# A hybrid decoder layer on one core: v's transposition leaves TensorE for VectorE blocks and DRAM transfers, and a head's delta rule starts at another step

## The chip, the cores and the metric

One core of one Trainium2 chip runs the whole program. The metric is the device time of one execution in microseconds. The kernel before takes 2156.06 us, the median of three runs that lie between 2155.36 and 2157.12 us.

## The reference, cut to what matters

One decoder layer works on 512 prompt tokens and 8 single sample tokens of width 2048. The part that the change touches is the prompt's gated delta rule: 8 heads of 128 columns, of which q, k and v come out of one input projection, a short causal convolution over time and a SiLU.

```python
qkv_c, new_conv = short_conv(conv_buf, qkv, conv_w)      # 4 taps over time, then silu
q = l2norm(q) * (DN_HEAD_DIM ** -0.5)
k = l2norm(k)
...
def step(S, xs):                                          # chunk by chunk, in order
    q_i, k_i, u_i, w_i, g_i, qk_i = xs
    v_new = u_i - jnp.einsum('bhck,bhkv->bhcv', w_i, S)
    o = (jnp.einsum('bhck,bhkv->bhcv', q_i * jnp.exp(g_i)[..., None], S)
         + jnp.einsum('bhcs,bhsv->bhcv', qk_i, v_new))
    S = S * jnp.exp(g_last)[..., None, None] + jnp.einsum('bhck,bhcv->bhkv', k_dec, v_new)
    return S, o
```

Beside it stand a pooling group, the output projection and a SwiGLU feed-forward network, whose matrices take most of the time. Everything is float32.

## The kernel before, in words

The program has a first phase up to about 605 us (input projection, convolution, delta rule, pooling) and then the output projection and the feed-forward network. Only the first phase is changed.

**Projection tiles.** `product` computes 128 columns of the input projection for all tokens. The weights are split into a high and a low part, and each of the 16 k tiles takes three matmuls for each of two halves of the tokens (lines 168 to 170, 256 or 264 columns wide): 96 matmuls a tile. The halves are skewed by three k tiles. The weights come in granules of eight k tiles: `raw` by DMA on SP's queue, `hi` cast on ScalarE (line 135), `lo` subtracted on VectorE (line 137), each with three buffers. `to_columns` (line 259) scales a finished half out of PSUM into `ext`; four VectorE operations (lines 737 and 739) make the convolution `y`, and ScalarE the SiLU (line 740).

**The weave.** Everything that is not a projection is cut into generators. `Weave.step()` is called after every k tile of a product from the fourth on and once at its end, 16 times a product; it advances up to four tracks. A generator yields how many steps its track then rests, and `add` takes the steps it waits before it starts. A track runs its tasks strictly one after the other: track 0 has the delta rule and, after it, the sample tokens' work; track 1 gates, keys and the pooling products; track 2 the transpositions over DRAM; track 3 the gates of the output. TensorE's instructions stand in this hand-made order. On VectorE, ScalarE and GpSimd a scheduler sorts them by its own estimate of when they can run, and each engine works its list strictly in order.

**A head.** `qv_tiles(h)` makes q's tile, then v's. Five steps after q's tile, `query_rows` turns q by 32x32 blocks on VectorE (line 753) into `bt`, writes it to DRAM from GpSimd's queue, and six steps later reads it back with four transfers into `qk`, whose rows are tokens. ScalarE squares these rows (line 923) for q's norm. `delta(h)` is added after v's tile and starts one step later. In it `it` 0 to 2 build a triangular inverse `cur` (matmuls of line 870, VectorE's line 872). At `it` 1 TensorE turns v by four transposes (line 885), and VectorE multiplies the rows by `ik` out of PSUM into `vs` (line 887). Then four chunks follow in order. In each, TensorE makes `wp` from `R` (line 904), ScalarE copies it to `W` (906), TensorE makes `dp` from `W` (909), VectorE makes the state `S` (912 or 914), TensorE makes `kp` from `S` (897), and VectorE the next `R` (899). At the end `on` is made from PSUM (939), and six steps later `output_columns` turns it back with a block transposition (764), one transfer to DRAM and four from it, on the same track 2 and the same GpSimd queue. Heads 0 to 3 and 4 to 7 are two batches; after each come other tiles (keys, or the pool's).

**The end of the phase.** After head 7, eight `pool_tile` products follow, and under them track 0 runs head 7's delta rule, then the sample tokens. The last of these, `sample_out`, multiplies its result into `mixa` (line 1015). The output projection then halves `mixa` (line 203), splits 16 tiles into high and low (line 195), and multiplies them (lines 1176 to 1178).

Of the kernel before, what the change touches and what calls it, by code (L numbers as in the profile page):

```python
# [8 lines left out]
F32 = mybir.dt.float32  # L9
# [3 lines left out]
ALU = mybir.AluOpType  # L13
# [4 lines left out]
P = 128  # L18
# [3 lines left out]
SEQ = 512  # L22
NTOK = NB + SEQ
H = 8
NCH = 4
# [8 lines left out]
HG = 8  # L34
BUFS = {
    "ext": 2, "y": 1, "ys": 1, "g3": 3, "junk": 1, "ss": 2, "rr": 2, "nb": 1, "u": 1, "tm": 2, "xt_": 1, "uu": 2,
    "qts": 1, "fq": 2, "aq": 1, "vs": 1, "bt": 2, "tq": 1, "R": 2, "W": 2, "S": 2, "so": 2, "ro": 2, "s0": 2, "s2": 1, "kd": 4, "st": 2,
}
SKEW = 3
AHEAD = 2000  # L40
# [29 lines left out]
def decoder_kernel(ctx, tc, x_prompt, x_sample, state_delta, state_conv, state_pool, norm_mix, w_in,  # L70
# [4 lines left out]
    te, act, dve, pool, sp = nc.tensor, nc.scalar, nc.vector, nc.gpsimd, nc.sync  # L75
# [12 lines left out]
    def pst():  # L88
        return ps_dn.tile([P, 512], F32, tag="dn", name="dn")
# [31 lines left out]
    weave = Weave()  # L121
# [399 lines left out]
    with ExitStack() as p1:  # L521
# [4 lines left out]
        def d1tile(tag, shape, name, dtype=F32):  # L526
            return (pre if tag == "ext" else d1).tile(shape, dtype, tag=tag, name=name, bufs=BUFS[tag])
# [192 lines left out]
        def v3(a):  # L720
            return a.rearrange("p (c j) -> p c j", c=NCH)

        def bc3(a):
            return a.rearrange("p (c o) -> p c o", o=1).broadcast_to([P, NCH, P])

        def ck(c):
            return slice(P * c, P * (c + 1))
# [12 lines left out]
            act.activation(out, y, AF.Silu)  # L740
            pool.tensor_copy(ccp[:, :, t], ext[:, SEQ:SEQ + 3])

        tok_d = dram.tile([2, H, P, SEQ], F32, name="tok_d")

        def by_chunk(a):
            return a.rearrange("p (i c q) -> p c i q", i=4, c=NCH)

        def by_column(a):
            return a.rearrange("p (i q) -> p i q", i=4)

        def query_rows(h, qT):
            bt, d = d1tile("bt", [P, SEQ], "bt"), tok_d[0, h]
            dve.transpose(bt.rearrange("p (j c q) -> p c j q", j=4, c=NCH), qT.rearrange("p (c j q) -> p c j q", j=4, c=NCH))
            pool.dma_start(d, bt)
            yield 6
            rows = d.rearrange("(i p) (j f) -> j p i f", p=32, j=4)
            qk = qks[h] = d1tile("tq", [P, SEQ], "qk")
            for j in range(4):
                pool.dma_start(qk[32 * j:32 * j + 32, :].rearrange("p (n q) -> p n q", n=4), rows[j])

        def output_columns(h, on):
            bt = d1tile("bt", [P, SEQ], "bt")
# [80 lines left out]
            yield 1  # L843


        def delta(h, qT, vT):
            kT, nn, kd = mixb[:, h % 4, 0:SEQ], mixb[:, 4 + h % 4, 0:SEQ], kds[h]
            fk, ik = sck[:, h, 0, :], sck[:, h, 1, :]
            utf = utfs[h % 2]
            udf, tdf = utf[:, 0], utf[:, 1]  # L850
            gcb, dm = decay(h)
            act.activation(gcb, gcb, AF.Exp)
            qts = d1tile("qts", [P, SEQ], "qts")
            dve.tensor_tensor(qts, qT, gcb, op=ALU.mult)

            xp = pst()
            for c in range(NCH):
                te.matmul(xp[:, P * c:P * c + 96], nn[:, ck(c)], tdf[:, c, 0:96], start=True, stop=True)  # L860
            xt_ = d1tile("xt_", [P, NCH, 96], "xt_")
            act.copy(xt_, v3(xp)[:, :, 0:96])
            cur = d1tile("uu", [P, SEQ], "uu")
            pool.tensor_copy(v3(cur), udf)
            yield 2
            for it in range(3):
                yp = v3(pst())
                j = slice(32 * it + 32, P)
                for c in range(NCH):
                    te.matmul(yp[0:96, c, j], xt_[:, c, :], udf[:, c, j] if it == 0 else v3(cur)[:, c, j],  # L870
                              start=True, stop=True)
                dve.scalar_tensor_tensor(v3(cur)[0:96, :, j], yp[0:96, :, j], -1.0, udf[0:96, :, j],
                                         op0=ALU.mult, op1=ALU.add)
                if it == 0:
                    gq_ = pst()
                    for c in range(NCH):
                        te.matmul(gq_[:, ck(c)], kT[:, ck(c)], qT[:, ck(c)], start=True, stop=True)
                    aq = d1tile("aq", [P, SEQ], "aq")
                    for c in range(NCH):
                        dve.scalar_tensor_tensor(aq[:, ck(c)], gq_[:, ck(c)], fk[:, c:c + 1], dm[:, ck(c)],  # L880
                                                 op0=ALU.mult, op1=ALU.mult)
                if it == 1:
                    vtp = pst()
                    for c in range(NCH):
                        te.transpose(vtp[:, ck(c)], vT[:, ck(c)], ident)
                    vs = d1tile("vs", [P, SEQ], "vs")
                    dve.tensor_tensor(v3(vs), v3(vtp), bc3(ik), op=ALU.mult)
                yield 2

            op_ = pst()  # L890
            S = None
            for c in range(NCH):
                if S is None:
                    R = vs[:, ck(c)]
                else:
                    kp = pst()
                    te.matmul(kp[:, 0:P], kT[:, ck(c)], S, start=True, stop=True)
                    Rt = d1tile("R", [P, P], "R")
                    dve.scalar_tensor_tensor(Rt, kp[:, 0:P], negc[:, c, h:h + 1], vs[:, ck(c)],
                                             op0=ALU.mult, op1=ALU.add)  # L900
                    R = Rt
                    yield 2
                wp = pst()
                te.matmul(wp[:, 0:P], cur[:, ck(c)], R, start=True, stop=True)
                W = d1tile("W", [P, P], "W")
                act.copy(W, wp[:, 0:P])
                yield 2
                dp = pst()
                te.matmul(dp[:, 0:P], kd[:, ck(c)], W, start=True, stop=True)
                S2 = d1tile("S", [P, P], "S")  # L910
                if S is None:
                    dve.tensor_copy(S2, dp[:, 0:P])
                else:
                    dve.scalar_tensor_tensor(S2, S, egl[:, c, h:h + 1], dp[:, 0:P], op0=ALU.mult, op1=ALU.add)
                    te.matmul(op_[:, ck(c)], qts[:, ck(c)], S, start=True, stop=False)
                te.matmul(op_[:, ck(c)], aq[:, ck(c)], W, start=(S is None), stop=True)
                S = S2
                yield 1
                if c == 0:
                    ss = d1tile("ss", [P, NCH], "ss")  # L920
                    junk = d1tile("junk", [P, P], "junk")
                    for j in range(NCH):
                        act.activation(by_column(junk), by_chunk(qks[h])[:, j], AF.Square, accum_out=ss[:, j:j + 1])
# [11 lines left out]
            dve.tensor_scalar(so, so, 1.0 / P, EPS, op0=ALU.mult, op1=ALU.add)  # L935
# [179 lines left out]
        def qv_tiles(h):  # L1115
            utf = utfs[h % 2].rearrange("p a c j -> p (a c) j")
            for q in range(4):
                r = slice(32 * q, 32 * q + 32)
                sp.dma_start(utf[r, :, r], ud_d[h, q].rearrange("a c s j -> s (a c) j"))
            qT = d1tile("s0", [P, SEQ], "qT")  # L1120
            qkv_tile(0, h, qT)
            weave.add(query_rows(h, qT), 2, 5)
            vT = d1tile("s2", [P, SEQ], "vT")
            qkv_tile(2, h, vT)
            weave.add(delta(h, qT, vT), 0, 1)

        kds, qks = {}, {}
        for b in range(2):
# [17 lines left out]
        splits = {}  # L1146
# [11 lines left out]
        for t in (6, 7, 4, 5, 2, 3, 0, 1):  # L1158
            pool_tile(t, operands)
            if t % 2:  # L1160
                weave.add(pool_mix(t // 2, *splits[t // 2]), 1, 20 if t == 7 else 12 if t > 1 else 7)
        weave.add(pool_out(), 0, 6)

        order = [*range(8), 14, 15, 12, 13, 10, 11, 8, 9]
# [939 lines left out]
```

## Time and profile before

| what | value |
|---|---|
| median of 3 runs | 2156.06 us (2155.36 to 2157.12) |
| the profiled execution | 2156.18 us, span 2154.4 us |
| TensorE busy, of the span | 99% |
| VectorE, ScalarE, GpSimd busy | 82%, 43%, 22% |
| granted TensorE clock | 1.00 |

TensorE's row is full from the first slices to the end. Its matmuls overlap, so a matmul "of 0.28 us" starts 0.12 us after the one before it: what an instruction costs TensorE is read from the starts of its neighbours, not from its own length. Waits of the other engines cost nothing by themselves as long as TensorE's next instruction has its operands.

### The profile page before, as it was taken

What the parts mean: (1) busy time and instruction counts of PE and PEld (TensorE: products, weight loads), DVE (VectorE), ACT (ScalarE), POOL (GpSimd) and SP (SyncE); (2) the same over time, 40 slices, a digit from 0 to 9 for tenths busy, and PEclk for the clock granted to TensorE, in tenths of its full rate; (3) what the DMA queues carried; (4) which work ended last, traced back from release to release, by engine and by line L of the source; (5) the groups of instructions that cost most, each with busy time, mean ns of one, the idle gap of its engine ahead of it and who ended that gap; (6) DMA issues with size and microseconds to landing.
All of it is one profiled execution on the core that took longest, in us unless ns stands there. A gap on an engine that the chain in (4) does not pass through costs nothing.

```text
span 2154.4 us, 43035 instructions
## 1 busy us (share of the span) xinstructions
PE 2129.6 (99%) x17745; PEld 2121.1 (98%) x17745; DVE 1759.6 (82%) x2635; ACT 929.0 (43%) x1404; POOL 481.9 (22%) x592
## 2 busy tenths in 40 slices
PE   8999999999999999999999999999999999999998
PEld 7999999999999999999999999999999999999998
DVE  7786767666599979888888888888887897887997
ACT  6533452433255454434434434434334444435444
POOL 2112320231012202333233233232113302003100
PEclk9999999999999999999999999999999999999999
DMA  8344434443445534454455455454456746438333
GB/s 282 92 121 110 116 103 117 115 117 98 128 126 166 152 105 124 144 170 144 137 172 147 134 172 147 134 172 133 118 148 195 228 111 205 115 104 247 93 108 119
DMA packets 445826, 305.44 MB, mean 142 GB/s; under 512 B 27836, under 2 KB 424533, under 8 KB 442285
## 3 DMA queue, kind: packets, MB, share of 16 engines
q1 hardware_dynamic: 422733, 219.94, 36.5%
q0 software_dynamic: 21584, 81.95, 12.0%
q8 instruction: 139, 2.28, 0.4%
q10 hardware_dynamic: 1312, 0.80, 0.1%
q14 instruction: 58, 0.48, 0.1%
HBM read 255.66 MB, written 47.63 MB: 141 GB/s over the span
## 4 chain that ended last, share of the span: by engine, by line
PE 85%; DVE 8%; DMA 2%; ACT 2%; issue 2%; POOL 1%; DVEq 0%; ACTq 0%; POOLq 0%; SPq 0%
PE dn L1250 21%; PE dn L1249 21%; PE dn L1251 21%; PE mm L168 6%; PE mm L170 5%; PE mm L169 5%; DVE lo L1243 1%; DVE lo L137 1%; PE dn L870 1%; DMA st<-a_d 1%; DVE raw L1271 1%; POOL st L1803 0%; DVE tm L836 0%; PE dn L986 0%; DVE u L838 0%
## 5 line engine op out<-in xcount | busy, mean ns | idle before, releaser
L1243 DVE TENSOR_TENSOR lo<-raw,hi 128x1024 fp32r<-128x1024 f32 (+1 forms) x422 | 528.6, 1272 | 89.5 <-ACT hi L1242 87.4
L1242 ACT CAST hi<-raw 128x1024 fp32r<-128x1024 f32 (+1 forms) x422 | 427.5, 1027 | 402.9 <-DVE raw L1271 204.2
L168 PE MATMUL mm<-xh,hi 128*128 128x256 f32 (+1 forms) x1280 | 379.5, 297 | 2.6 <-DVE mixa L259 2.6
L169 PE MATMUL mm<-xl,hi 128*128 128x256 f32 (+1 forms) x1280 | 361.6, 283 | 0.9 <-DVE xl L350 0.5
L170 PE MATMUL mm<-xh,lo 128*128 128x256 f32 (+1 forms) x1280 | 361.7, 283 | 0.4 <-DVE lo L137 0.4
L168 PEld LDWEIGHTS mm<-xh,hi 128*128 128x128 f32 x1280 | 241.4, 189 | 3.8 <-DVE mixa L259 3.2
L169 PEld LDWEIGHTS mm<-xl,hi 128*128 128x128 f32 x1280 | 241.7, 189 | 1.7 <-DVE xl L350 1.7
L170 PEld LDWEIGHTS mm<-xh,lo 128*128 128x128 f32 x1280 | 240.9, 188 | 0.6 <-DVE lo L137 0.6
L1271 DVE TENSOR_TENSOR raw<-raw 128x1024 f32<-128x1024 f32 (+1 forms) x130 | 174.6, 1343 | 2.2
L1250 PE MATMUL dn<-b21l,hi 128*128 128x260 f32 x620 | 175.8, 284 | 0.4 <-DVE b21l L1813 0.4
L1251 PE MATMUL dn<-b21h,lo 128*128 128x260 f32 x620 | 175.4, 283 | 0.0
L1249 PE MATMUL dn<-b21h,hi 128*128 128x260 f32 x620 | 174.9, 282 | 0.0
L1251 PE MATMUL dn<-b11h,lo 128*128 128x260 f32 x612 | 173.2, 283 | 1.4 <-DVE lo L1243 1.4
L1250 PE MATMUL dn<-b11l,hi 128*128 128x260 f32 x612 | 173.3, 283 | 0.0
L1249 PE MATMUL dn<-b11h,hi 128*128 128x260 f32 x612 | 172.7, 282 | 0.0
L1435 POOL TENSOR_TENSOR mixa<-mixa 128x520 f32<-128x520 f32 x22 | 51.3, 2330 | 495.5 <-DVE mixa L1429 495.5
L1249 PE MATMUL dn<-T1h,hi 128*128 128x260 f32 x556 | 158.1, 284 | 0.0
L1250 PE MATMUL dn<-T1l,hi 128*128 128x260 f32 x556 | 157.7, 284 | 0.0
L1251 PE MATMUL dn<-T1h,lo 128*128 128x260 f32 x556 | 156.7, 282 | 0.0
L1249 PE MATMUL dn<-B22h,hi 128*128 128x260 f32 x548 | 155.9, 284 | 0.0
L1250 PE MATMUL dn<-B22l,hi 128*128 128x260 f32 x548 | 155.6, 284 | 0.0
L1251 PE MATMUL dn<-B22h,lo 128*128 128x260 f32 x548 | 154.6, 282 | 0.4 <-DVE lo L1243 0.4
(663 smaller groups left out, 6504.0 us busy)
## 6 DMA issues: line engine op xcount, KB each, us to landing
raw<-in_w_gate_up_dram SPq DMA_DIRECT2D x134, 512.0 KB
raw<-in_w_in_dram SPq DMA_DIRECT2D x79, 512.0 KB
a_d<-mixa POOLq DMA_DIRECT2D x22, 1040.0 KB, 5.5
raw<-in_w_down_dram SPq DMA_DIRECT2D x48, 448.0 KB
mixb<-in_w_gate_up_dram SPq DMA_DIRECT2D x41, 512.0 KB
raw<-in_w_out_dram SPq DMA_DIRECT2D x25, 512.0 KB
st<-a_d POOLq DMA_DIRECT2D x49, 260.0 KB, 6.8
raw<-in_w_down_dram SPq DMA_DIRECT2D x24, 512.0 KB
```

The costliest lines, as they stand in the source:

```text
L137: dve.tensor_tensor(lo[:, r], raw[:, r], hi[:, r].bitcast(F32), op=ALU.subtract)
L168: te.matmul(acc[ci], wh, hi[k][:, c0:c1], start=(k == 0), stop=False)
L169: te.matmul(acc[ci], wh, lo[k][:, c0:c1], start=False, stop=False)
L170: te.matmul(acc[ci], wl, hi[k][:, c0:c1], start=False, stop=(k == len(w) - 1))
L870: te.matmul(yp[0:96, c, j], xt_[:, c, :], udf[:, c, j] if it == 0 else v3(cur)[:, c, j], start=True, stop=True)
L1242: act.copy(hi, raw)
L1243: dve.tensor_tensor(lo, raw, hi.bitcast(F32), op=ALU.subtract)
L1249: te.matmul(acc, wh[:, k, :], xf[:, k, :], start=start and k == 0, stop=False)
L1250: te.matmul(acc, wh[:, k, :], xg[:, k, :], start=False, stop=False)
L1251: te.matmul(acc, wl[:, k, :], xf[:, k, :], start=False, stop=stop and k == wh.shape[1] - 1)
L1271: dve.tensor_tensor(r[name], r[a], r[b], op=op)
L1435: pool.tensor_tensor(q[:, 4:8:2, :], q[:, 1:4:2, :], q[:, 0:2, :], op=ALU.subtract)
```

## The change

v's tile goes ahead of q's. `query_rows` becomes `token_rows(kind, h, src, dst)`, and v goes through it too: a block transposition, one transfer to a third plane of `tok_d`, and four transfers back, now into `vs` itself, whose SiLU output they overwrite. The four transposes on TensorE and their PSUM bank are gone. The multiplication by `ik` is done in place in SBUF at `it` 1 (`scaled`). `vs` is laid out by column blocks, so the first `wp` and the `R` of later chunks read it in four pieces of 32 columns. `vs` has two buffers. The delta rule starts eight weave steps after q's tile instead of one after v's, and the pool product of the first pool pair waits 34 steps in place of 20.

```diff
-    "qts": 1, "fq": 2, "aq": 1, "vs": 1, ...
+    "qts": 1, "fq": 2, "aq": 1, "vs": 2, ...
-        tok_d = dram.tile([2, H, P, SEQ], F32, name="tok_d")
+        tok_d = dram.tile([3, H, P, SEQ], F32, name="tok_d")
+        def scaled(a, s):
+            a = a.rearrange("p (i c q) -> p i c q", i=4, c=NCH)
+            dve.tensor_tensor(a, a, s.rearrange("p (o c u) -> p o c u", o=1, u=1).broadcast_to([P, 4, NCH, 32]),
+                              op=ALU.mult)
-        def query_rows(h, qT):
-            bt, d = d1tile("bt", [P, SEQ], "bt"), tok_d[0, h]
-            dve.transpose(bt.rearrange(...), qT.rearrange(...))
+        def token_rows(kind, h, src, dst):
+            bt, d = d1tile("bt", [P, SEQ], "bt"), tok_d[kind, h]
+            dve.transpose(bt.rearrange(...), src.rearrange(...))
             pool.dma_start(d, bt)
             yield 6
             rows = d.rearrange("(i p) (j f) -> j p i f", p=32, j=4)
-            qk = qks[h] = d1tile("tq", [P, SEQ], "qk")
+            if dst is None:
+                dst = qks[h] = d1tile("tq", [P, SEQ], "qk")
             for j in range(4):
-                pool.dma_start(qk[32 * j:32 * j + 32, :].rearrange("p (n q) -> p n q", n=4), rows[j])
+                pool.dma_start(dst[32 * j:32 * j + 32, :].rearrange("p (n q) -> p n q", n=4), rows[j])
 ...
                 if it == 1:
-                    vtp = pst()
-                    for c in range(NCH):
-                        te.transpose(vtp[:, ck(c)], vT[:, ck(c)], ident)
-                    vs = d1tile("vs", [P, SEQ], "vs")
-                    dve.tensor_tensor(v3(vs), v3(vtp), bc3(ik), op=ALU.mult)
+                    scaled(vs, ik)
 ...
-                    R = vs[:, ck(c)]
+                    R = by_chunk(vs)[:, c]
-                    dve.scalar_tensor_tensor(Rt, kp[:, 0:P], negc[:, c, h:h + 1], vs[:, ck(c)],
-                                             op0=ALU.mult, op1=ALU.add)
+                    dve.scalar_tensor_tensor(by_column(Rt), by_column(kp[:, 0:P]), negc[:, c, h:h + 1],
+                                             by_chunk(vs)[:, c], op0=ALU.mult, op1=ALU.add)
 ...
+            vs = d1tile("vs", [P, SEQ], "vs")
+            qkv_tile(2, h, vs)
+            weave.add(token_rows(2, h, vs, vs), 2, 5)
             qT = d1tile("s0", [P, SEQ], "qT")
             qkv_tile(0, h, qT)
-            weave.add(query_rows(h, qT), 2, 5)
-            vT = d1tile("s2", [P, SEQ], "vT")
-            qkv_tile(2, h, vT)
-            weave.add(delta(h, qT, vT), 0, 1)
+            weave.add(token_rows(0, h, qT, None), 2, 5)
+            weave.add(delta(h, qT, vs), 0, 8)
 ...
-                weave.add(pool_mix(t // 2, *splits[t // 2]), 1, 20 if t == 7 else 12 if t > 1 else 7)
+                weave.add(pool_mix(t // 2, *splits[t // 2]), 1, 34 if t == 7 else 12 if t > 1 else 7)
```

The changed kernel's lines stand three higher in the delta rule (line 915 is the old 912) and seven higher where q is turned.

**VectorE, the first chunk of head 1.** Before, from the last step of the inverse (`uu`) to the first `R`; `S` is the state after chunk 0, `lo` a weight granule, `mixa` the gate of the head before:

```order
L872 SCALAR_TENSOR_TENSOR uu<-dn,utf_647 96x4x32
L927 TENSOR_SCALAR fq<-fq 128x4
L933 TENSOR_TENSOR ro<-fq 128x4
L137 TENSOR_TENSOR lo<-raw,hi 128x1024
L944 SCALAR_TENSOR_TENSOR mixa<-mixb,prm,mixa 128x512
L912 COPY S<-dn 128x128
L899 SCALAR_TENSOR_TENSOR R<-dn,negc,vs 128x128
```

and now:

```order
L879 SCALAR_TENSOR_TENSOR uu<-dn,utf_647 96x4x32
L259 TENSOR_TENSOR ext<-mm,rb 128x256
L737 TENSOR_SCALAR y<-ext,prm 128x512
L137 TENSOR_TENSOR lo<-raw,hi 128x1024
L739 SCALAR_TENSOR_TENSOR y<-ext,prm,y 128x512
L927 TENSOR_SCALAR ss<-ss 128x4
L739 SCALAR_TENSOR_TENSOR y<-ext,prm,y 128x512
L915 COPY S<-dn 128x128
L739 SCALAR_TENSOR_TENSOR y<-ext,prm,y 128x512
L930 TENSOR_SCALAR fq<-fq 128x4
L902 SCALAR_TENSOR_TENSOR R<-dn,negc,vs 128x128
```

Between the inverse and `S` now stand an eviction, three of the four convolution operations of the next head's v, a weight granule, and `ss`, which needs ScalarE's squares of `qk`. Heads 1, 2, 3, 5 and 6 have this order; head 7 has the pool's additions in place of the convolution. On TensorE the distance from the matmul of `dp` to that of `kp`, which reads `S`, is 6 projection matmuls before and now; from the first `wp` to `dp` it was 12 and is 21.

**GpSimd, one head.** The transfers of head 1 before (`qk` is head 2's q, `mixb` head 1's output):

```order
L754 DMA tok_d<-bt 128x512
L759 DMA qk<-tok_d 32x4x128 x4
L864 COPY uu<-utf_647 128x512
L215 TENSOR_TENSOR ro<-so,mhalf 128x4
L741 COPY ccp<-ext 128x3
L765 DMA tok_d<-bt 128x4x128
L769 DMA mixb<-tok_d 32x16x32 x4
L215 TENSOR_TENSOR fq<-ss,mhalf 128x4
```

and now (`qk` is head 1's q, `mixb` head 0's output, `vs` head 2's v):

```order
L215 TENSOR_TENSOR ro<-so,mhalf 128x4
L760 DMA tok_d<-bt 128x512
L772 DMA tok_d<-bt 128x4x128
L766 DMA qk<-tok_d 32x4x128 x4
L776 DMA mixb<-tok_d 32x16x32 x3
L741 COPY ccp<-ext 128x3
L776 DMA mixb<-tok_d 32x16x32
L215 TENSOR_TENSOR fq<-ss,mhalf 128x4
L263 MEMSET ext 128x3
L760 DMA tok_d<-bt 128x512
L766 DMA vs<-tok_d 32x4x128 x4
```

The order has five more transfers a head, and the write of the output stands between q's write and q's reads. In ScalarE's order the first two of the four squares of `qk` now stand, in all eight heads, ahead of a weight cast `hi` and of the first `W`; before they stood around the copy of `xt_`, ahead of the inverse.

**VectorE, the end of the phase.** From the sample tokens' last matmul (its result is read by the first row) to the product into `mixa`, before:

```order
L1012 TENSOR_SCALAR sc_u<-dn 128x64
L137 TENSOR_TENSOR lo<-raw,hi 128x1024
L220 RECIPROCAL sc_u<-sc_u 128x64
...
L259 TENSOR_TENSOR pe_7259<-mm,rb 128x256
L259 TENSOR_TENSOR pcs<-mm,rb 128x8
...
L1015 SCALAR_TENSOR_TENSOR mixa<-sc_u,prm,mixa 128x8x8
L203 TENSOR_TENSOR mixa<-mixa 128x4x260 x2
```

and now:

```order
L1015 TENSOR_SCALAR sc_u<-dn 128x64
...
L1077 TENSOR_TENSOR pes<-pe_7256 128x512
L137 TENSOR_TENSOR lo<-raw,hi 128x1024 x2
L220 RECIPROCAL sc_u<-sc_u 128x64
...
L1082 SCALAR_TENSOR_TENSOR pw<-pes,pe_7256 128x512
...
L195 TENSOR_TENSOR dl<-pw,dh 128x520
L1018 SCALAR_TENSOR_TENSOR mixa<-sc_u,prm,mixa 128x8x8
L203 TENSOR_TENSOR mixa<-mixa 128x4x260 x2
```

One pool addition, a second weight granule, `pw` and `dl` are now ahead of it, and on TensorE 102 projection and pool matmuls stand between that last sample matmul and the output projection, where it was 153.

More of the change, by code (lines that the diff above doesn't have):

```diff
@@ L36 @@
     "ext": 2, "y": 1, "ys": 1, "g3": 3, "junk": 1, "ss": 2, "rr": 2, "nb": 1, "u": 1, "tm": 2, "xt_": 1, "uu": 2,
-    "qts": 1, "fq": 2, "aq": 1, "vs": 1, "bt": 2, "tq": 1, "R": 2, "W": 2, "S": 2, "so": 2, "ro": 2, "s0": 2, "s2": 1, "kd": 4, "st": 2,
+    "qts": 1, "fq": 2, "aq": 1, "vs": 2, "bt": 2, "tq": 1, "R": 2, "W": 2, "S": 2, "so": 2, "ro": 2, "s0": 2, "s2": 1, "kd": 4, "st": 2,
 }
@@ L749, in by_column @@
             return a.rearrange("p (i q) -> p i q", i=4)
-        def query_rows(h, qT):
-            bt, d = d1tile("bt", [P, SEQ], "bt"), tok_d[0, h]
-            dve.transpose(bt.rearrange("p (j c q) -> p c j q", j=4, c=NCH), qT.rearrange("p (c j q) -> p c j q", j=4, c=NCH))
+        def scaled(a, s):
[4 more added lines that the diff above has]
+            bt, d = d1tile("bt", [P, SEQ], "bt"), tok_d[kind, h]
+            dve.transpose(bt.rearrange("p (j c q) -> p c j q", j=4, c=NCH), src.rearrange("p (c j q) -> p c j q", j=4, c=NCH))
             pool.dma_start(d, bt)
@@ L843, in eliminate, with delta @@
             yield 1
-        def delta(h, qT, vT):
+        def delta(h, qT, vs):
             kT, nn, kd = mixb[:, h % 4, 0:SEQ], mixb[:, 4 + h % 4, 0:SEQ], kds[h]
```

## The prediction

> **What bounds the kernel now.** I read the page first, then the waits and the windows of the first phase, then its order of time engine by engine.
>
> ```profile
> span 2154.4 us, 43035 instructions
> PE 2129.6 (99%) x17745; PEld 2121.1 (98%) x17745; DVE 1759.6 (82%) x2635; ACT 929.0 (43%) x1404; POOL 481.9 (22%) x592
> ...
> sum 465.00, PE 463.65 PEld 462.66 DVE 320.59 ACT 181.15 POOL 94.76; mean PE 115.91 PEld 115.67 DVE 80.15 ACT 45.29 POOL 23.69
> ...
> PE dn L870 <- ACT xt__2146 L862: 0.7, 1, 0.7
> PE dn L870 <- DVE uu L872: 0.5, 1, 0.5
> PEld dn L870 <- ACT xt__4960 L862: 0.3, 1, 0.3
> ```
>
> TensorE is busy 463.65 of the 465 us from 140 to 605 us, all that the change reorders (third row, a sum over four windows). The three waits below it, 1.5 us together, are at the inverse of heads 0, 7 and 4. So a microsecond comes off only with TensorE's own work or with these waits, and comes on wherever TensorE now has to wait. TensorE's order is fixed by hand: a late operand stops everything behind it.
>
> **What is removed.** Four transposes a head, 32 in all.
>
> ```profile
> 199.51 0.81 PE L870 MATMUL dn<-uu,xt__2535 128*96 128x64 f32 x8
> 200.16 0.61 PE L885 MATMUL dn<-ident,vT 128*128 128x128 f32 x4
> 200.53 0.37 PE L168 MATMUL mm<-xh,hi 128*128 128x264 f32 x1
> 202.04 0.79 PE L870 MATMUL dn<-uu,xt__2535 128*96 128x32 f32 x8
> 202.67 0.37 PE L168 MATMUL mm<-xh,hi 128*128 128x264 f32 x1
> ```
>
> With them the next projection matmul starts 1.02 us after L870 (200.53 - 199.51); without them, at the next `it`, 0.63 us (202.67 - 202.04). The four start within 0.37 us (200.16 to 200.53), and I take this: 8 x 0.37 = 3.0 us off. The Trainium skill's page "TensorE: Matmul & The Clock Gate" (Part 4: PE-mode transpose) gives about 275 ns for a transpose in a kernel's context, for bf16; 32 of these would be 8.8 us and the time 5.8 us lower than my sum. The row here agrees with it as a length (0.61 us for four that overlap) but not as a cost, since the neighbours' starts bound it.
>
> The three waits: the delta rule now begins inside a tile and not one step behind it, where evictions, convolution and SiLU crowd. I take all 1.5 us off; bounds 0 and 1.5.
>
> **What is added off TensorE's path.** A block transposition of v (0.71 us, L753 below) and a multiplication SBUF to SBUF.
>
> ```profile
> L887 DVE TENSOR_TENSOR vs<-dn,sck x8: 676/692/692, 169.5 to 487.0; 128x512 f32<-128x512 f32 x8
> 220.65 0.99 DVE L854 TENSOR_TENSOR qts<-qT,gcb 128x512 f32<-128x512 f32 x1
> 221.68 1.10 DVE L778 SCALAR_TENSOR_TENSOR dm<-gcb,gcs,mneg 128x128 f32<-128x128 f32 x3
> ```
>
> The trace has no such multiplication. The nearest row is the same one out of PSUM, 0.69 us, which it replaces; I take 0.69, bounds 0.48 (L737 below, one tensor read) and 0.99 (L854, two of SBUF). The first `wp` reads `vs` in pieces, which no row shows: bounds 0 and as long again, 0.38 a head (L904 below), 3 us in all; I take 0, since 32 columns in a row stay together. On GpSimd five transfers, about 2.8 us a head (0.62 and 4 x 0.55, L754 and L759 below); it is busy 94.76 of 465 us and has room. All this costs nothing by itself; what counts is what stands behind it in order.
>
> **The moved step: `S` at chunk 0.** Take as zero the last matmul of the next head's v tile, where the first `wp` now stands.
>
> ```profile
> 204.19 0.38 PE L904 MATMUL dn<-vs,uu 128*128 128x128 f32 x2
> 205.85 0.38 PE L909 MATMUL dn<-W,kd 128*128 128x128 f32 x2
> 207.01 0.38 PE L897 MATMUL dn<-S,mixb 128*128 128x128 f32 x2
> ...
> 209.45 0.42 DVE L259 TENSOR_TENSOR ext<-mm,rb 128x256 f32<-128x256 f32 x1 [1.14 <-PE mm L170]
> 209.79 0.34 DVE L914 SCALAR_TENSOR_TENSOR S<-S,egl,dn 128x128 f32<-128x128 f32 x1
> 210.04 0.48 DVE L737 TENSOR_SCALAR y<-ext,prm 128x512 f32<-128x512 f32 x1
> 210.44 1.22 DVE L137 TENSOR_TENSOR lo<-raw,hi 128x1024 fp32r<-128x1024 f32 x1
> 211.57 0.75 DVE L739 SCALAR_TENSOR_TENSOR y<-ext,prm,y 128x512 f32<-128x512 f32 x1
> 212.24 0.35 DVE L899 SCALAR_TENSOR_TENSOR R<-dn,negc,vs 128x128 f32<-128x128 f32 x1
> 214.73 0.71 DVE L753 STREAM_TRANSPOSE bt<-qT 128x512 f32<-128x512 f32 x1 [0.70 <-ACT qT L740]
> ```
>
> TensorE needs `S` for `kp` at: first `wp` to `dp` 1.66 us with 12 matmuls between (first two rows), and 9 more matmuls at 0.12 make 2.7; `dp` to `kp` 1.16 (third row). That is 3.9 us. VectorE, by starts of neighbours: it begins 0.2 behind the tile's last matmul; eviction 0.35, first `y` 0.4, `lo` 1.13, `y` 0.67, `ss` 0.15, `y` 0.67, `S` 0.3: ready at 3.9. So without any further wait the chain just fits where before it had room. But `lo` needs its cast, and ScalarE's order has two squares of `qk` ahead of that cast:
>
> ```profile
> 203.55 1.05 ACT L135 CAST hi<-raw 128x1024 fp32r<-128x1024 f32 x1 [4.34 <-PE mm L169]
> 224.97 0.30 ACT L923 ACTIVATE junk<-qk 128x128 f32<-128x128 f32 x1
> 225.18 0.19 ACT L923 ACTIVATION_READ_ACCUMULATOR junk<-qk 128x1 f32 x1
> ...
> 215.74 0.62 POOL L754 DMA_DIRECT2D tok_d<-bt  x1 [1.49 <-DVE bt L753]
> 218.40 0.56 POOL L759 DMA_DIRECT2D qk<-tok_d  x1 [2.05 <-DMA tok_d<-bt]
> 219.39 1.64 POOL L759 DMA_DIRECT2D qk<-tok_d  x3 [0.42 <-issue]
> 223.35 1.04 POOL L215 TENSOR_TENSOR ro<-so,mhalf 128x4 f32<-128x4 f32 x1 [1.24 <-DVE so L935]
> ...
> DMA to landing us min/median/max: 2.1/2.7/4.1
> ```
>
> When do the rows of `qk` land? From the start of q's write to the first read 2.7 us (215.74, 218.40), the fourth read starts 1.6 later, landing 2.7 (the median of the last row; 2.1 to 4.1): 7.0 behind the write. The write starts 0.3 behind the end of q's block transposition (214.73 + 0.71, 215.74). That transposition stands, in the new order, behind the whole end of the head before: from q's last matmul eviction 0.6, the wait for a cast and `lo` 2.0, four convolution operations 2.4, `S` 0.3, small ones 0.4, GpSimd's root with its way there and back 1.4, `on` 0.6, the block 0.7: 8.4 us. q's last matmul lies 16.1 before zero (the tile of v between, 96 matmuls or 11.5, and 4.6 of delta's own matmuls). So `qk` lands at -16.1 + 8.4 + 0.3 + 7.0 = -0.4. Two squares (0.4 each with the accumulator) and the cast (1.0) end at 1.4, and `lo` may start at 1.5 instead of 0.95: `S` at 4.5, a wait of 0.6 us on TensorE.
>
> It meets heads 1, 2, 3, 5, 6 and 7. Heads 0 and 4 have no head's end in front of them, so their `qk` is early and `ss` or `lo` no wait. 6 x 0.6 = 3.6 us on. Bounds: 0 (landing at the minimum, 2.1, and no delay by ScalarE), and 2.0 a head (landing at 4.1), 12 us in all.
>
> The front of the chain is tight too: VectorE's first `uu` (0.5) comes behind q's block, `qts` (1.0), the output's block (0.65), four `dm` (1.4) and a `lo` (1.13): it ends 4.7 behind a block that ends at -7.7, so at -3.0, and `it` 1, which lies 15 matmuls (1.9 with what they lose at the joins) and two steps of the inverse (0.65 and 0.63) ahead of zero, asks for it at -3.2. I add 0.1 for four heads, 0.4 us; bounds 0 and 0.5 a head.
>
> **The moved end of the phase.** Track 0 ends seven steps later.
>
> ```profile
> 584.86 0.33 PE L1010 MATMUL dn<-sc_u,ones 128*128 128x64 f32 x2
> 603.48 0.28 PE L1176 MATMUL mm<-xh,hi 128*128 128x260 f32 x1
> ...
> 588.87 0.28 DVE L1015 SCALAR_TENSOR_TENSOR mixa<-sc_u,prm,mixa 128x64 f32<-128x64 f32 x1
> 589.18 2.39 DVE L203 TENSOR_TENSOR mixa<-mixa 128x1040 f32<-128x1040 f32 x2
> 595.02 0.69 DVE L1079 SCALAR_TENSOR_TENSOR pw<-pes,pe 128x512 f32<-128x512 f32 x1
> 597.46 3.14 DVE L195 TENSOR_TENSOR xl<-mixa,xh 128x520 fp32r<-128x520 f32 x5
> ```
>
> From the sample's last matmul to the output projection it is 18.6 us with 153 matmuls, 0.12 each; now 102, so 12.4. VectorE's part from that matmul to the product into `mixa` takes 4.0 now (588.87 - 584.86); in the new order another `lo` (1.1), a pool addition (0.65), `pw` (0.65) and `dl` (0.6) stand in it, 3.0 in all: 7.0. Halving 2.35, then `lo` 1.1, and the splits of 0.62 among two evictions, two pool operations and a small `lo`: the fifth split ends at 16.3. TensorE wants the k tiles from 12.4 on, the fifth 1.8 later, 14.2. That is a wait of 2.1, and some 0.4 more for later tiles. I take 2.5 us; bounds 0 and 5. Before, the fifth was done at about 599.3 and wanted at 605.3, so 6 us of room go, as the steps say.
>
> **The sum.** The profiled execution took 2156.18 us, its span 2154.4; the 1.8 us around the span I leave as they are, and it lies 0.1 above the median. 2156.2 - 3.0 - 1.5 + 3.6 + 0.4 + 2.5 = 2158.2: **2158 us**, a change of +0.1%, inside the 0.2% (4.3 us) that a measurement of this kernel can tell from none.
>
> **The rivals.**
>
> *`qk` later still: slower.* One mechanism: q's reads now stand behind the write of the output on GpSimd's queue, and that behind VectorE's second block. If they land at the maximum, 4.1 instead of 2.7, `S` is 1.4 later in six heads: 8.4 us more, 2166.6. It decides from a landing 0.4 us later than I reckon (2.4 us more, over the bound of 0.2%). For it: 256 KB of output travel on the same queue at that moment. Against: the write is mostly over when the reads start. 0.20.
>
> *v's rows late: slower.* VectorE's `scaled` stands in order ahead of q's last eviction. v's block comes after the first `R` and the gate, about 6.9 behind zero; 0.3 + 7.0 puts the rows at 14.2, and VectorE reaches `scaled` at about 14.4. If the rows land 1.0 later than that, all of q's chain and `S` move by 1.0: 6 more, 2164. For it: no slack; against: it only shifts. 0.10.
>
> *Everything fits: faster.* If `S` keeps up and the end has room, only -4.5 is left: 2151.7. For it: before the change TensorE waited next to nothing on chains as dense; against: the counts of rows above. 0.10.
>
> *GpSimd's issues are held up.* If each read waits for a VectorE instruction as long as `lo`, 1.2 us, four reads come 4.8 later: 6 x 4.8 = 29, 2187. Against it:
>
> ```profile
> L759 POOL DMA_DIRECT2D qk<-tok_d x32: 548/549/577, 159.1 to 474.5; - x32
> ```
>
> 548 to 577 ns for 32 issues, beside a VectorE that is busy 320.59 of 465 us. The Trainium skill has this rule on "SBUF — State Buffer" (SBUF: two separate sides): GpSimd can't write descriptors while VectorE holds the shared port. By that rule such issues stretch; this trace shows none that did. 0.03.
>
> **Chances and range.** The forecast, with its own bounds, 0.57; the rivals 0.20, 0.10, 0.10, 0.03. Faster by more than 0.2% is the third rival: 0.10. Slower is the first, the second and the fourth, 0.33, and 0.02 of the forecast's upper edge: 0.35. The same: 0.55. The range 2151.5 to 2167 takes in both ends; beyond it lie the fourth rival and the worse half of the first two.
>
> **What would show it.** In the profile after: no transposes of v on TensorE and a head of about 31.5 us where it was 31.3; TensorE's L900 (`kp`) waiting about 0.6 us for `S` of L915 in six heads; ScalarE's L926 waiting for `qk`; no wait at the inverse of heads 0, 4 and 7; TensorE waiting some 2.5 us for `xl` around 600 us. No wait at L900, or one above 1.5 us, makes the third step wrong; a wait at L877 or L912 (`W`) would be one that I placed elsewhere.

## The result: 1.0% slower, and the profile after

The changed kernel takes 2177.76 us (median of five runs, 2175.48 to 2182.11), the kernel before 2155.95 us beside it. The ratio is 1.0101, with a 95% interval of 1.009 to 1.0113: 21.8 us slower, where the prediction had 2158 us and a range to 2167. The profiled execution of the changed kernel took 2175.48 us; it is the fastest of the five.

The page after (first two rows), the window from 140 to 605 us (third row, its sums by engine; TensorE had 463.65 us there before), and the waits of TensorE, a row being "who waits <- for whom: us in total, times, longest":

```profile
span 2173.7 us, 43032 instructions
PE 2133.0 (98%) x17713; PEld 2122.4 (98%) x17713; DVE 1762.3 (81%) x2643; ACT 925.5 (43%) x1402; POOL 512.7 (24%) x632
...
sum 465.00, PE 448.92 PEld 445.35 DVE 305.14 ACT 164.62 POOL 122.03; mean PE 448.92 PEld 445.35 DVE 305.14 ACT 164.62 POOL 122.03
...
PE dn L900 <- DVE S L915: 8.4, 8, 1.3
PE dn L912 <- ACT W L909: 4.9, 4, 2.4
PE mm L1181 <- DVE xl L195: 2.3, 2, 1.2
PE dn L907 <- DVE uu L879: 1.4, 1, 1.4
PE dn L989 <- DMA s<-in_state_delta_dram: 1.3, 2, 0.8
```

TensorE waits for `S` in all eight heads and, ahead of that, for `W` in four. The waits for `xt_` and `uu` at the inverse (L877 now) are gone. What the other engines did in head 1 shows why. From the timeline, GpSimd (q's write, the output's write, q's four reads), then SyncE, ScalarE, VectorE and TensorE:

```profile
201.17 0.61 POOL L760 DMA_DIRECT2D tok_d<-bt  x1 [1.84 <-DVE bt L759]
202.36 0.77 POOL L772 DMA_DIRECT2D tok_d<-bt  x1 [0.58 <-DVE bt L771]
203.81 2.20 POOL L766 DMA_DIRECT2D qk<-tok_d  x4 [0.67 <-DMA tok_d<-bt]
...
203.98 0.38 SPq L131 DMA_DIRECT2D raw<-in_w_in_dram  x1
...
210.46 0.31 ACT L926 ACTIVATE junk<-qk 128x128 f32<-128x128 f32 x1 [5.06 <-DMA qk<-tok_d]
211.21 1.03 ACT L135 CAST hi<-raw 128x1024 fp32r<-128x1024 f32 x1
212.14 0.26 ACT L909 COPY W<-dn 128x128 f32<-128x128 f32 x1
...
212.27 1.23 DVE L137 TENSOR_TENSOR lo<-raw,hi 128x1024 fp32r<-128x1024 f32 x1 [3.04 <-ACT hi L135]
214.86 0.28 DVE L915 COPY S<-dn 128x128 f32<-128x128 f32 x1
...
208.07 0.38 PE L907 MATMUL dn<-vs,uu 128*128 128x128 f32 x2
212.45 0.49 PE L912 MATMUL dn<-W,kd 128*128 128x128 f32 x2 [1.48 <-ACT W L909]
215.20 0.49 PE L900 MATMUL dn<-S,mixb 128*128 128x128 f32 x2 [1.32 <-DVE S L915]
```

ScalarE stands idle for 5.06 us at the first square of `qk`. Its cast and the first `W` stand behind two squares, VectorE's `lo` behind the cast, and `S` behind `lo`. This is the prediction's chain, but the rows of `qk` land 2.3 us after the first `wp` (208.07), and not 0.4 before it.

The last row of the following fence is the landing of these four reads after their issue; the rows above it are, before the change, the reads of head 6's q, SyncE's next weight load and the landing of those reads:

```profile
441.33 2.19 POOL L759 DMA_DIRECT2D qk<-tok_d  x4 [2.02 <-DMA tok_d<-bt]
443.45 0.37 SPq L131 DMA_DIRECT2D raw<-in_w_in_dram  x1
DMA to landing us min/median/max: 2.1/2.1/2.3
...
DMA to landing us min/median/max: 3.7/4.9/5.0
```

Before, the weight load of 512 KB went out 2.1 us after the first of these reads; after, 0.17 us after it (203.81, 203.98). In all eight heads after the change a weight load goes out between 0.8 us ahead and 0.2 us behind the first read. The load goes into the buffer that `lo` has read: in each head it is issued within 0.05 us of the end of a `lo`, and `lo` stands in the new order just where the reads do. Before, a weight load went out so near the first read in heads 0 and 4 alone, whose reads took 3.0 to 4.1 us; head 7's, beside a state load of the sample, took 3.1 to 4.1.

A second thing was in no part of the prediction: the granted clock. TensorE in four stretches of 3.41 us of head 5 (stretch, length, busy us and instructions, granted clock, share of the DMA engines, GB/s):

```profile
442.53:445.94 3.41, 1.43 (x10) 1.00 0.00 0
445.94:449.35 3.41, 2.46 (x11) 0.50 0.58 159
449.35:452.76 3.41, 3.41 (x18) 0.50 0.20 77
452.76:456.17 3.41, 3.41 (x32) 1.00 0.19 58
```

TensorE waits for `W` (2.4 us) and then for `S` (1.3 us) in that head, and its clock is halved for 6.8 us from within the second wait (445.94) on. From `kp` to the 36th matmul behind it the starts take 6.99 us there and 4.36 us in heads 1, 2, 3 and 6, so the half clock costs 2.6 us.

### The profile page after: what moved, and what is told of

It is laid out like the page before. It is cut to its first block, busy times and chain, and to the rows that moved or that the text cites. A ratio compares the mean times of both kernels' runs of the same rounds, so it can differ in the third digit from the quotient of the medians.

```text
span 2173.7 us, 43032 instructions
## 1 busy us (share of the span) xinstructions
PE 2133.0 (98%) x17713; PEld 2122.4 (98%) x17713; DVE 1762.3 (81%) x2643; ACT 925.5 (43%) x1402; POOL 512.7 (24%) x632
## 3 DMA queue, kind: packets, MB, share of 16 engines
q8 instruction: 139, 2.28, 0.4%
## 4 chain that ended last, share of the span: by engine, by line
PE 73%; DVE 7%; DMA 4%; issue 2%; ACT 1%; POOL 1%; DVEq 0%; ACTq 0%; POOLq 0%
PE dn L1254 21%; PE dn L1253 21%; PE dn L1255 21%; PE mm L168 3%; PE mm L170 3%; PE mm L169 3%; DVE lo L1247 1%; DMA qk<-tok_d 1%; DMA st<-a_d 1%; DVE y L739 1%; DVE lo L137 1%; DMA tok_d<-bt 1%; DMA vs<-tok_d 1%; PE mm L1253 0%; PE mm L1254 0%
```

## The experiments

**e1: the squares out of the way.** Only where the squares of `qk` may start is changed. Their scratch tile takes a buffer of `R`, which is free only when the second `wp` has read it.

```diff
-                if c == 0:
+                if c == 2:
                     ss = d1tile("ss", [P, NCH], "ss")
-                    junk = d1tile("junk", [P, P], "junk")
+                    junk = d1tile("R", [P, P], "junk")
```

> The changed kernel, with the four squares of qk on ScalarE held back: their scratch tile is taken from the two buffers of R, so that they cannot start before the second wp has read its R, and on ScalarE they now stand behind the cast, behind the first two W and behind the SiLU of v. Theory (qk's rows land too late, and what stands behind the squares on ScalarE and VectorE is late with them): the waits of TensorE for W at L912 (4.9 us) go, those for S at L900 (8.4 us) shrink to about 1, the half-clock stretch at 446 us (3.4 us) goes with them: about 2159 us, 2155 to 2164. Rival (the delta rule's place alone: lo and the convolution stand ahead of S on VectorE, qk or not): the waits at L900 stay near 1 us a head, 2167 to 2173.

Measured: 2159.81 us (ten runs), ratio 1.0014 to before (1.0005 to 1.0024), 18.0 us faster than the changed kernel. TensorE's waits and the landing of `qk`:

```profile
PE mm L1181 <- DVE xl L195: 2.3, 2, 1.2
...
PE dn L989 <- DMA s<-in_state_delta_dram: 1.2, 2, 0.6
PE dn L907 <- DVE uu L879: 0.8, 1, 0.8
DMA to landing us min/median/max: 2.7/4.5/6.0
```

By starts, no wait for `W` is left and 0.2 us a head for `S`, and there is no half clock in the phase, although the rows land as late as in the changed kernel. So the place of the delta rule is not what costs most: `S`, behind an eviction, `lo` and the convolution, is almost in time when `lo` is not held up by the squares.

**e2: the order alone.** e1 with v turned by TensorE again and no transfers of v.

```diff
-                    scaled(vs, ik)
+                    vtp = pst()
+                    for j in range(NCH):
+                        te.transpose(vtp[:, ck(j)], vs[:, ck(j)], ident)
+                    vs = d1tile("vs", [P, SEQ], "vs")
+                    dve.tensor_tensor(v3(vs), v3(vtp), bc3(ik), op=ALU.mult)
...
-            weave.add(token_rows(2, h, vs, vs), 2, 5)
```

> As e1, but v is transposed by TensorE again (four transposes a head, as before the change) and has no transfers: what is left of the change is v's tile ahead of q's and the delta rule 8 steps behind q's tile. Theory (v's transfers cost nothing on TensorE's path once the squares are out of the way): e1 plus the transposes, 2.0 to 4.0 us, so about 2162. Rival (v's rows land late and VectorE stands at the multiplication L754, up to 2.0 us in the trace after): 2 to 8 us faster than e1, since that stall is gone with the transfers.

Measured: 2161.56 us (ten runs), ratio 1.0021 (1.0012 to 1.003), 1.75 us above e1. That is the side of the theory, a little under its 2.0 to 4.0. As a difference of two kernels the size is uncertain. The traces show the transposes' own price: from the matmuls ahead of them (L877) to the next projection matmul it is 1.01 us in every head of e2 and about 0.62 in e1, where they are missing. That makes 3.1 us in eight heads, as the prediction took it. The rival is excluded: without the stall of VectorE for v's rows the kernel is not faster.

**e3: without the output's transfers.** The five transfers of the output are left out.

```diff
             dve.transpose(bt, on)
-            pool.dma_start(d.rearrange("c p f -> p c f"), v3(bt))
             yield 6
-            rows = d.rearrange("c (i p) (j q) -> j p (c i) q", p=32, q=32)
-            for j in range(4):
-                pool.dma_start(on[32 * j:32 * j + 32, :].rearrange("p (n q) -> p n q", q=32), rows[j])
```

> The changed kernel without the five transfers of a head's output (its write L772 and its four reads L776; VectorE's block stays): the output of the delta rule is then left unturned, which is the part of the computation that is left out. Theory A (qk's reads wait behind the output's traffic on GpSimd's queue): their landing falls from the median of 4.4 us to under 3, the waits for W and S mostly go, about 2160 us. Theory B (they share the DMA engines with SyncE's transfers, which come at the same moment: 512 KB of weights, 256 KB of gcb and the small pieces of utf): the landing stays at 3.8 us or more and the time at 2170 to 2178.

Measured: 2172.19 us (four runs). The landing of `qk` and two waits of TensorE:

```profile
DMA to landing us min/median/max: 2.3/4.3/4.9
...
PE dn L900 <- DVE S L915: 6.9, 6, 1.3
...
PE dn L912 <- ACT W L909: 1.4, 4, 0.6
```

The median is 4.3 us, and 4.4 in the changed kernel: the output's traffic on GpSimd's queue is not the cause of the late landing. It adds a little behind it: the waits for `W` are 3.5 us shorter without it, those for `S` 1.5.

**e4: the delta rule 14 steps behind q's tile.**

```diff
-            weave.add(delta(h, qT, vs), 0, 8)
+            weave.add(delta(h, qT, vs), 0, 14)
```

> The changed kernel with the delta rule 14 steps behind q's tile, not 8: the rows of qk have about 4.5 us more before the squares stand in the way. Theory (qk late): the waits for W and S go (about 15 us with the half-clock stretch 18), and the sample's last step and the output projection's wait for xl come some 4 us later (6 steps of 0.72): about 2164 us, 2159 to 2169. Rival (the new order of the tiles is what costs, wherever the delta rule begins): 2172 or more, with waits at other joins.

Measured: 2165.22 us (four runs), ratio 1.004 (1.0025 to 1.0055): the theory's number. The reads now go out 1.0 to 2.4 us ahead of a weight load in six of the eight heads, and they land in 2.8 us (median). But `S` of later chunks (L917) is late by 0.5 us in five heads, and TensorE waits 2.9 us for `xl` at the end, with 6.8 us of half clock behind that (from 608.62), which the theory had not counted.

**e5: an eighth of the weight load.** The 512 KB loads for the tiles of q and v become 64 KB; the casts and `lo` keep their size and the squares their place.

```diff
+                if thin:
+                    load(slice(0, 1))
+                    r8 = raw[:, 0:P].rearrange("p (o c) -> p o c", o=1).broadcast_to([P, n, P])
+                    h8, l8 = (x[:, :f].rearrange("p (k c) -> p k c", k=n) for x in (hi, lo))
+                    act.copy(h8, r8)
+                    dve.tensor_tensor(l8, r8, h8.bitcast(F32), op=ALU.subtract)
```

> The changed kernel with the same orders on ScalarE, VectorE and TensorE, but each 512 KB load of weights for a tile of q or v fetches one eighth (64 KB, the first of its eight k tiles, which the cast and lo then read eight times): what is left out are seven eighths of those weights. In the traces so far a read of qk lands in 2.1 to 2.3 us when no weight load goes out within 1.5 us of it, and in 3.4 to 5.3 when one does; after the change one goes out within 0.8 us of the first read in all eight heads. Theory (the weight load shares the DMA engines with the reads): with it cut to an eighth the reads land in 2.1 to 3.0 us (median), and the waits for W and S shrink to under 5 us in all, 2158 to 2165 us. Rival (GpSimd's own queue, or the small pieces of utf and the 256 KB of gcb): the landing stays above 3.5 and the time above 2170.

Measured: 2169.45 us (four runs). The transfers around q's reads (size, median landing), in head 1 and then in head 2:

```profile
qk<-tok_d POOLq DMA_DIRECT2D x4, 64.0 KB, 2.4
gcb<-gcr_d SPq DMA_DIRECT2D x1, 256.0 KB
mixb<-tok_d POOLq DMA_DIRECT2D x3, 64.0 KB, 3.6
utf<-ud_d SPq DMA_DIRECT2D x3, 32.0 KB
raw<-in_w_in_dram SPq DMA_DIRECT2D x1, 64.0 KB
...
raw<-in_w_in_dram SPq DMA_DIRECT2D x1, 512.0 KB
qk<-tok_d POOLq DMA_DIRECT2D x4, 64.0 KB, 4.0
gcb<-gcr_d SPq DMA_DIRECT2D x1, 256.0 KB
```

The landing follows the theory and the time does not, and both have one reason. The load that meets q's reads fetches weights for more than a tile ahead. In heads 0, 1, 4 and 5 these are for q or v and were cut; in heads 2, 3, 6 and 7 they are for the next keys or the pool and stayed at 512 KB. That gives a control within one run: medians of 2.3 to 2.6 us in the four heads with the small load, with `utf` and `gcb` still beside them, and of 2.9 to 4.2 in the four with the full one. TensorE's waits in heads 0 and 4 vanished, and that for `W` in head 5 fell from 2.5 to 0.7; but in heads 1 and 5 the fourth read still took 4.0 us and more, and the wait for `S` stayed at 1.5. So the weight load is shown to be what delays the first three reads. The fourth is late for another reason too, which was not taken apart. The 256 KB of `gcb` are a candidate: SyncE issues them within 0.4 us of the fourth read in heads 1 and 5, and 0.4 and 1.0 us behind it in heads 0 and 4, where it took 3.0 and 2.2.

The Trainium skill says on "DMA: Bandwidth & Descriptors" (Issuing engines are not separate DMA queues) that transfers run on the same 16 engines and interleave, whichever engine started them. The rows above agree: a load that SyncE started makes GpSimd's reads 1.6 us slower.

**e6: the sample earlier.** e1, and what stood between the last delta rule and the sample's products moves to track 2.

```diff
-        weave.add(conv_out())
-        weave.add(sample_norms())
+        weave.add(conv_out(), 2)
+        weave.add(sample_norms(), 2)
```

> e1 with the convolution's outputs and the sample's norms put beside the last delta rule (track 2) and not behind it: the sample's products and its last step come some 11 weave steps (8 us) earlier. Theory (the 2.9 us that TensorE waits for xl at the output projection are the sample's last step, 7 steps late): that wait goes, and the time is 2.9 us under e1, 2156.9 (2155 to 2158). Rival (the splits at the output projection are late for another reason, VectorE's pool tiles): no change, 2159.8.

Measured: 2155.24 us (eleven runs) beside 2156.32 of the kernel before, ratio 0.9993 (0.9984 to 1.0002): 4.6 us under e1. No wait for `xl` is left, and none for the sample's state loads (1.2 us in e1), which the expectation had not counted. This is the fastest of the kernels here, and it can't be told from the kernel before.

Why is it no faster, with the transposes and the three waits gone (4.8 us by starts)? The traces show where most of that goes. The first `kp` of each head still starts late behind `S`: its two matmuls start 0.34 and 0.21 us after the matmul before them in head 0, where it was 0.12 and 0.11 before. Over the eight heads that is 2.6 us, and one `uu` in head 3 costs 1.2.

**e7, e9, e10: other steps for the delta rule.** e6 with `weave.add(delta(h, qT, vs), 0, ...)` at 10, 7 and 6.

> e6 with the delta rule 10 steps behind q's tile instead of 8, which the earlier sample now leaves room for. Theory (with the delta rule 8 behind, S is just late at kp, 24 times 0.045 us, and the first uu once 0.8): up to 1.9 us under e6, 2155 to 2157. Rival (every further step of delay moves the stalls to other joins, as the 14 steps did, where S was late by 0.5 in five heads): 2157 to 2162.

> e6 with the delta rule 7 steps behind q's tile instead of 8. By the prediction's count S is ready just when kp wants it with 8 steps and undisturbed squares. Theory (that count): one step, 0.72 us, earlier makes S, or the first uu, late by up to 0.7 us in each of eight heads, 2156 to 2161 us. Rival (what matters is only how VectorE's and ScalarE's orders interleave with the tile, which they are sorted anew for each delay, as with 10 steps, which cost 10.9 us): 2164 or more, with waits at chunk 2 or 3, or no loss at all.

> e6 with the delta rule 6 steps behind q's tile instead of 8. Theory (the prediction's count): S or the first uu late by up to 1.4 us in each of eight heads, 2159 to 2167 us, more than with 7 steps. Rival (the interleaving of the orders decides, not the distance): no more than with 7 steps.

Measured: 2166.16 us at 10 steps (five runs, ratio 1.0042, 1.003 to 1.0055), 2162.60 at 7 (ten runs, 1.0024, 1.0014 to 1.0033), 2160.73 at 6 (ten runs, 1.0015, 1.0006 to 1.0024), and 2155.24 at 8. TensorE's longest waits at 10, at 7 and at 6 steps:

```profile
PE dn L900 <- DVE S L917: 3.2, 7, 0.5
PE dn L877 <- DVE uu L879: 2.4, 1, 2.4
...
PE dn L989 <- DMA s<-in_state_delta_dram: 2.4, 2, 1.2
PE dn L900 <- DVE S L915: 2.0, 8, 0.5
...
PE dn L989 <- DMA s<-in_state_delta_dram: 3.3, 2, 1.8
PE dn L877 <- ACT xt__6174 L869: 0.5, 1, 0.5
```

At 10 my theory falls, and the time lies above the rival's range too: later is not safer. `S` of a later chunk then stands behind a `lo`, as VectorE's timeline of head 5 at 10 steps shows:

```profile
442.17 1.23 DVE L137 TENSOR_TENSOR lo<-raw,hi 128x1024 fp32r<-128x1024 f32 x1 [0.40 <-ACT hi L135]
443.31 0.34 DVE L917 SCALAR_TENSOR_TENSOR S<-S,egl,dn 128x128 f32<-128x128 f32 x1
```

At 7 `S` is late in all eight heads, by 0.25 us on average and 0.5 at most, where the count allowed up to 0.7, and the state loads of the sample take about as much; the time lies between the ranges of theory and rival. At 6 `S` is in time again, as the rival has it, and the largest wait is the one for the state loads, 3.3 us, with 3.4 us of half clock behind its first part (from 526.60). So the distance in steps does not decide by itself. What goes with the times at 10 and 8 is how VectorE's list, which is sorted anew for each delay, interleaves `S` with `lo` and the convolution; at 7 and 6 a good part is the sample's state loads, and no run took the two apart.

**e8: how long a wait lowers the clock.** The kernel before, with S of chunk 1 multiplied by one, in place, 0 to 40 times.

```diff
                 S = S2
+                for _ in range((0, 8, 12, 16, 20, 26, 32, 40)[h] if c == 1 else 0):
+                    dve.tensor_scalar(S, S, 1.0, None, op0=ALU.mult)
                 yield 1
```

> The kernel before, with a chain of multiplications by one behind S of chunk 1, so that kp of chunk 2 waits: none in head 0, then 8, 12, 16, 20, 26, 32 and 40 of them, which by 0.15 us each makes one wait on TensorE of about 0.5 to 5 us in each of heads 1 to 7, with full work around it. It is to tell from what length one wait lowers the granted clock. After the change two waits of 2.4 and 1.3 us, 3 us apart, went ahead of 6.8 us at half clock, and 1.6 and 1.5 did not. Theory (a stretch of fixed length is judged by its idle share, more than half of some 3.4 us): half clock follows the waits of 2.4 us and more, for 3 to 7 us. Rival (only a wait that fills a stretch whole does it): none below 3.4 us.

Measured: 2228.1 us (one run). A multiplication cost 0.28 us and not 0.15, so the waits run from 3.9 to 12.8 us, and every one of the seven was followed by half clock, for 3.41 us after the shortest and 13.65 after the longest. None was short enough to find the limit. The traces of the other kernels narrow it. TensorE in three stretches of e3, at the one wait for `uu` of 1.6 us, and in the two stretches of the changed kernel around head 1's waits of 1.5 and 1.3 us:

```profile
274.69:278.10 3.41, 1.81 (x17) 1.00 0.45 126
278.10:281.51 3.41, 3.41 (x18) 0.50 0.25 84
281.51:284.92 3.41, 3.41 (x31) 1.00 0.53 151
...
210.42:213.83 3.41, 1.93 (x15) 1.00 0.37 54
213.83:217.24 3.41, 2.09 (x18) 1.00 0.56 154
```

All half-clock stretches inside these programs last a multiple of 3.41 us and, within one run, lie on one grid of that pitch (in e8 they start at 116.11 and at whole multiples of the pitch after that). The rise of the granted clock at the start of each program and its fall at the end lie on the same grid, so the grid is known in all twelve runs. Over these, every window at full clock with 1.34 us of TensorE's work or less was followed by half clock, and none with 1.93 us or more was. Of the eight windows in between four were: those with 1.43 us (after), 1.57 (e2), 1.81 (e3) and 1.90 (e10) were followed by half clock, and those with 1.46 (the kernel before, at its end), 1.62 (e3, at its end), 1.63 (e8) and 1.80 (e1) were not.

So the halving goes with the work that is summed in one window, without a sharp limit by this measure. Parts of two waits that fall into one window count together, as in head 5 above. One wait across the edge of two windows can pass: e7's wait of 2.4 us for `uu` left 2.44 and 2.03 us of work in its two windows, and the clock stayed full. This is read off the traces; no run was made to move a wait across an edge. It agrees with the theory on e8 in its kind, not in its limit of 2.4 us for a wait.

The Trainium skill has this window on "TensorE: Matmul & The Clock Gate" (Part 1: The HAM clock gate): 3413 ns, free-running. The grid here agrees. Its advice to avoid idle gaps above some 3 us (Why this matters for your kernels) is too mild for this case: 1.6 us in one gap was enough in e3.

## Why the prediction was wrong, point by point

The step that failed is the landing of `qk` in "the moved step". The prediction had the reads start 4.7 us ahead of the first `wp` and land 4.3 us later (1.6 and the median of 2.7). They do start 3.9 to 5.7 ahead, 4.8 on average. The last of them lands 4.9 to 6.9 later, since a read takes 4.4 us in the median and not 2.7. What stood behind that was right for the six heads that it was reckoned for: with the prediction's own rows a landing at L makes `S` late by L + 1.0 us.

| head | last read of `qk` lands, from the first `wp` | L + 1.0 | waits for `W` and `S`, by starts |
|---|---|---|---|
| 1 | +2.28 | 3.28 | 3.12 |
| 2 | +1.47 | 2.47 | 2.30 |
| 3 | +0.41 | 1.41 | 1.25 |
| 5 | +3.05 | 4.05 | 4.01 |
| 6 | +0.84 | 1.84 | 1.71 |
| 7 | +0.25 | 1.25 | 1.10 |

The last column is each gap between matmul starts less the usual 0.12 us. With heads 0 and 4 (1.21 and 0.70, where L + 1.0 would be 2.1 and 1.5) it makes 15.4 us where the sum had 3.6.

Term by term, in us, measured by starts in the traces (before against after where no other run is named):

| term | sum had | measured |
|---|---|---|
| 32 transposes | -3.0 | -3.1 (e2 against e1) |
| three waits at the inverse | -1.5 | all gone, -1.7 by starts |
| `W` and `S`, chunk 0 | +3.6 | +15.4 |
| first `uu` | +0.4 in four heads | +1.5 in one |
| xl at the end | +2.5 | +2.9 |
| half clock | none | +2.6 |
| the sample's state loads | none | +1.3 |

The right column makes +18.9, and the spans differ by 19.3 (2173.7 - 2154.4).

- **The price of a landing was a median over two kinds of read.** The row 2.1/2.7/4.1 held reads that met a weight load and reads that did not. Which kind the new order makes was in reach: the load is released by `lo`, and `lo` stands in the new order beside q's reads. I asked what stood on GpSimd's queue and not what SyncE would issue in that microsecond.
- **The rival "`qk` later still"** is what happened, with the wrong cause: it blamed the output's write on GpSimd's queue, and e3 shows that the landing stays without it. Its worst case, 4.1 us, was the largest landing before, while six of eight heads go above it in their median.
- **Heads 0 and 4** were said to have no wait. Their reads go out 5.2 and 5.7 us ahead of the first `wp`, hardly earlier than the others' (3.9 to 5.2), and TensorE waits 1.2 and 0.7 us.
- **The wait for `W`** was not placed. `W` stands on ScalarE behind the same squares and cast, so a late landing is felt first there; e1 removes it together with that for `S`.
- **The half clock** is a price of waits that the sum did not know. It turned the worst head's 4.0 us into 6.6.
- **"v's rows late"**: VectorE does stand up to 2.0 us at `scaled`, but e2, which has no such stall, is not faster than e1. **"GpSimd's issues are held up"**: q's four reads are issued in 2.2 us, as before. **"Everything fits"**: e6, with the squares and the sample moved as well, comes near it, 22.5 us below the changed kernel but not down to the 2151.7 of this rival, since `S` is still a little late.
- **Right**: the transposes, the removed waits, the reads' issue, the chain from the squares to `S`, `xl` at the end, and nearly that without the squares `S` is just in time at 8 steps (0.2 us late in each head of e1).

## What to carry to other kernels

A transfer's time to landing is no constant of its row: split the row by what else is issued in the same microsecond, and ask of a moved step which loads of other queues it will now meet. Work that waits for a transfer and isn't urgent must not stand, in an engine's in-order list, ahead of work that is: here four squares, which in e1 run some 9 us later and hold up none of this, held up the cast, `W` and `S`. And a wait on TensorE is paid a second time when it leaves too little work in one window of the clock: 2.6 us on top of 4.0 in head 5.

## What was not expected of the hardware

- TensorE's clock is halved in pieces of 3.41 us, on a fixed grid: always after a window with 1.34 us of work or less, never after one with 1.93 us or more, and in four of eight cases between. A single gap of 1.6 us was enough in e3, and one of 2.4 us across two windows was not in e7. What decides between 1.43 and 1.90 us is unexplained.
- Reads of 64 KB from GpSimd's queue land in 2.3 to 2.6 us (medians by head in e5) when a load of 64 KB of weights goes out beside them, and in 2.9 to 4.2 us beside one of 512 KB from SyncE. The fourth read of a head can be late beside the small load too (4.0 and 4.1 us in two heads).
- Ten, eight, seven and six steps between q's tile and the delta rule give no monotonous curve (2166.2, 2155.2, 2162.6 and 2160.7 us): the scheduler's order on VectorE changes with each, and 8 was the best of those tried.
